# Feed-forward part and output projection of a hybrid layer by 2 x 2 blocks in seven half-size products, with weight sums made by DMAs

## The chip, the cores and the metric

One Trainium2 chip, one core of it. The metric is the device time of one execution in microseconds, the median of several runs. A core has a matrix engine (TensorE, PE in the profile; the loading of its stationary operand is listed apart as PEld), VectorE (DVE), ScalarE (ACT), GpSimd (POOL) and SyncE (SP). Each takes its instructions in order and waits on semaphores for the others. DMAs are issued from the stream of an engine, here nearly all from SP (kind "hardware_dynamic" in the list of queues) and some from POOL ("software_dynamic").

## The reference

One layer, depth 1, in fp32, on 2048 prompt tokens and 8 x 4 decode tokens, width 1024, feed-forward width 3072:

```
xn   = rms_norm(x, g_mix_norm);  proj = xn @ w_in
mix  = concat(pooling mixer, RG-LRU recurrence, cross-attention into 256 memory tokens), each rms-normalised
x    = x + (mix * g_mix_out) @ w_out                       # 1024 x 1024
xn   = rms_norm(x, g_ffn_norm)
gate = xn @ w_ff_gate;  up = xn @ w_ff_up                  # 1024 x 3072 each
gate = gelu(causal depthwise conv of width 3 over gate)
x    = x + (gate * up) @ w_ff_down                         # 3072 x 1024
y    = rms_norm(x, g_final)
```

The states of the pooling, the convolutions and the recurrence are outputs too. The three products of the feed-forward part hold most of the arithmetic.

## The kernel before

**Arithmetic.** Activations lie with the channel on the 128 partitions and the token on the free axis. An fp32 product is made of three: both operands are split into a high part that the matrix engine's fast fp32 form takes whole and a low rest (`split`, L123 on ACT for the high part, L124 on VectorE or GpSimd for the rest), and `acc3` (L219 to L223) adds hi*hi, hi*lo and lo*hi into one PSUM tile.

**Tiling.** The 2080 columns are 6 pieces of 344, 344 and four times 348, taken in 3 blocks b of two pieces. A matmul has a 128 x 128 piece of a weight as its stationary operand and one piece of columns as the moving one.

**Stages.** First the recurrent group (input projection, convolution, gates, recurrence) of all 6 pieces, to some 290 us; then pooling and cross-attention, to some 530 us; the results lie in DRAM as mix. The output projection of block 0 covers the end of these groups (478 to 558 us). Then for each block: the output projection (blocks 1 and 2), the residual, the norm, and a loop over 24 chunks f of 128 feed-forward channels. A chunk loads 512 KB each of `w_gate`, `w_up`, `w_down` on SP and splits them 1024 wide, makes 48 matmuls for the gate and 48 for the up product, the conv on VectorE (L1042, L1047, L1054), the gelu on ACT, and the product of both (`hp`). The norm factor is multiplied in after the products, so these start without it. The 8 steps of the down product of a chunk (6 matmuls each) are kept in a list and popped between the matmuls of the next chunk; each adds its PSUM tile into `y` on VectorE (L893).

**The end.** The last chunk goes by halves of the columns (`last_down`), so that the norm and the stores of the first half run under the second.

**What sets the order.** Matmuls and SP's loads run in the written order; in the first two groups a weaver places background steps by a table of times `W`, which the change does not touch. The order on VectorE, ACT and POOL is chosen by the framework's scheduler from its own estimates, and a DMA issued from POOL is an instruction in POOL's order: if it has to wait for an earlier DMA, what stands behind it on POOL waits too.

## Time and profile before

| | |
|---|---|
| median of 3 runs | 2374.73 us (2374.39 to 2375.63) |
| span of the profiled execution | 2372.1 us |
| PE busy | 2298.0 us, 97%, 14370 matmuls |
| VectorE busy | 1640.9 us, 69% |
| ScalarE busy | 724.8 us, 31% |
| GpSimd busy | 484.5 us, 20% |
| moved by DMA | 195.88 MB, 83 GB/s over the span |
| granted clock of PE, mean | 0.986 |

The time of the profiled execution itself is not listed apart from its span; the median of the runs is 2.6 us above the span, which I take as what lies around it. In the rows below, a group of instructions shows `out<-in`, the count, the busy time and the mean of one in ns, then the idle time of that engine just before them and what ended it. A row of windows gives for a stretch of the span the busy time and the number of instructions of each engine, then the granted clock (1.00 is full), the share of time that the 16 DMA engines were busy, and GB/s.

### The profile page before, as it was taken

How to read it: one execution, taken by the hardware profiler on the slowest of the kernel's cores; microseconds unless marked ns; L12 is line 12 of the kernel's file. 1: busy time of each engine (PE TensorE's matmuls, PEld its weight loads, DVE VectorE, ACT ScalarE, POOL GpSimd, SP SyncE). 2: the span in 40 equal slices, each digit the busy share in tenths (PEclk: the TensorE clock that was granted, in tenths of full speed). 3: DMA queues.
4: the chain of work that ended last, by engine and by line, in shares of the span. 5: the costliest groups of instructions: out<-in, count | busy, mean ns of one | idle time of the engine just before them, and what ended most of it. 6: DMA issues, size and time to landing. Idle time of an engine off the chain costs nothing.

```text
span 2372.1 us, 34512 instructions
## 1 busy us (share of the span) xinstructions
PE 2298.0 (97%) x14370; PEld 2242.8 (95%) x14370; DVE 1640.9 (69%) x2404; ACT 724.8 (31%) x1016; POOL 484.5 (20%) x438
## 2 busy tenths in 40 slices
PE   8899889999999999999999999999999999999997
PEld 7888788889999999999999999999999999999996
DVE  8897886766666666666676666666658666666666
ACT  6646554644212212123421221212143121221212
POOL 3332343322111111101411011111132111111112
PEclk9899999999999999999999999999999999999998
DMA  4012332144222222224332222222163222222201
GB/s 157 26 49 81 117 148 82 61 146 128 70 72 72 63 79 65 71 63 150 103 109 69 72 63 75 68 72 72 35 195 111 72 72 63 72 64 79 71 20 49
DMA packets 60124, 195.88 MB, mean 83 GB/s; under 512 B 6832, under 2 KB 15776, under 8 KB 59968
## 3 DMA queue, kind: packets, MB, share of 16 engines
q1 hardware_dynamic: 55488, 177.96, 23.9%
q0 software_dynamic: 4336, 15.64, 1.7%
q8 instruction: 112, 1.84, 0.3%
q14 instruction: 44, 0.36, 0.1%
q10 hardware_dynamic: 144, 0.09, 0.0%
HBM read 175.17 MB, written 18.49 MB: 82 GB/s over the span
## 4 chain that ended last, share of the span: by engine, by line
PE 78%; DVE 14%; issue 3%; ACT 2%; POOL 2%; DMA 1%; DVEq 0%; SPq 0%; ACTq 0%; POOLq 0%
PE pu L223 22%; PE pd L223 22%; PE pg L223 22%; PE po L223 5%; PE pq L223 2%; DVE xc L511 2%; DVE alr L129 1%; PE pg L437 1%; DVE xc L508 1%; DVE xc L538 1%; DVE e L614 1%; DVE qu L801 1%; PE pf L223 1%; DVE y L907 1%; DVE m L606 1%
## 5 line engine op out<-in xcount | busy, mean ns | idle before, releaser
L893 DVE TENSOR_TENSOR y<-pd,y 128x696 f32<-128x696 f32 (+1 forms) x568 | 497.4, 876 | 422.5 <-PE pd L223 422.0
L223 PE MATMUL pd<-hh,h_wd 128*128 128x348 f32 (+1 forms) x1152 | 279.8, 323 | 2.8 <-DVE y L893 1.2
L223 PE MATMUL pg<-aha,l_wg 128*128 128x348 f32 (+1 forms) x1152 | 278.8, 322 | 0.0
L223 PE MATMUL pg<-aha,h_wg 128*128 128x348 f32 (+1 forms) x1152 | 278.7, 322 | 0.0
L223 PE MATMUL pu<-aha,h_wu 128*128 128x348 f32 (+1 forms) x1152 | 278.6, 322 | 0.0
L223 PE MATMUL pd<-hh,l_wd 128*128 128x348 f32 (+1 forms) x1152 | 278.6, 322 | 0.0
L223 PE MATMUL pg<-ala,h_wg 128*128 128x348 f32 (+1 forms) x1152 | 278.2, 321 | 0.0
L223 PE MATMUL pd<-hl,h_wd 128*128 128x348 f32 (+1 forms) x1152 | 277.4, 321 | 0.7 <-DVE hl L124 0.6
L223 PE MATMUL pu<-aha,l_wu 128*128 128x348 f32 (+1 forms) x1152 | 277.6, 321 | 0.0
L223 PE MATMUL pu<-ala,h_wu 128*128 128x348 f32 (+1 forms) x1152 | 277.0, 320 | 0.0
L1041 POOL COPY halo<-gt 128x2 f32<-128x2 f32 x72 | 67.2, 934 | 1002.1 <-DVE gt L1039 991.6
L123 ACT ACTIVATE h_wu<-st_wu 128x1024 fp32r<-128x1024 f32 x72 | 76.4, 1061 | 484.4 <-PE pg L223 483.6
L223 PEld LDWEIGHTS pd<-hh,h_wd 128*128 128x128 f32 x1152 | 200.2, 188 | 4.9 <-DVE y L893 1.8
L223 PEld LDWEIGHTS pd<-hl,h_wd 128*128 128x128 f32 x1152 | 199.9, 188 | 1.5 <-DVE hl L124 1.5
L223 PEld LDWEIGHTS pg<-ala,h_wg 128*128 128x128 f32 x1152 | 200.9, 189 | 0.0
L223 PEld LDWEIGHTS pu<-ala,h_wu 128*128 128x128 f32 x1152 | 200.6, 189 | 0.0
L223 PEld LDWEIGHTS pd<-hh,l_wd 128*128 128x128 f32 x1152 | 200.4, 188 | 0.0
L223 PEld LDWEIGHTS pu<-aha,h_wu 128*128 128x128 f32 x1152 | 200.1, 188 | 0.0
L223 PEld LDWEIGHTS pg<-aha,l_wg 128*128 128x128 f32 x1152 | 200.0, 189 | 0.0
L223 PEld LDWEIGHTS pg<-aha,h_wg 128*128 128x128 f32 x1152 | 199.7, 188 | 0.0
L223 PEld LDWEIGHTS pu<-aha,l_wu 128*128 128x128 f32 x1152 | 199.1, 188 | 0.0
L1056 ACT ACTIVATE cv<-cv,pv 128x696 f32<-128x696 f32 (+2 forms) x73 | 63.4, 868 | 431.8 <-DVE cv L1047 304.3
(337 smaller groups left out, 4049.4 us busy)
## 6 DMA issues: line engine op xcount, KB each, us to landing
st_wg<-in_w_gate_dram SPq DMA_DIRECT2D x72, 512.0 KB, 3.6
st_wu<-in_w_up_dram SPq DMA_DIRECT2D x72, 512.0 KB, 3.6
st_wd<-in_w_down_dram SPq DMA_DIRECT2D x72, 512.0 KB, 3.6
st_wo<-in_w_out_dram SPq DMA_DIRECT2D x24, 512.0 KB, 5.4
xr<-in_x_dram SPq DMA_DIRECT2D x8, 696.0 KB, 4.7
xp<-in_x_dram SPq DMA_DIRECT2D x8, 696.0 KB, 5.6
y<-in_x_dram SPq DMA_DIRECT2D x16, 348.0 KB, 5.5
st_wr<-in_w_in_dram SPq DMA_DIRECT2D x7, 512.0 KB, 4.6
```

What stands on the lines that cost most here:

```text
L123: S.activation(out=hi, in_=src, func=AF.Copy)
L129: V.scalar_tensor_tensor(out=lo, in0=src, scalar=g, in1=hi.bitcast(F32), op0=ALU.mult, op1=ALU.subtract)
L223: T.matmul(o, w_[:, ks], z, start=(k == 0 and i == 0), stop=(k == nk - 1 and i == 2))
L437: T.matmul(pg[:, 0:n], bdg[:, 4 * d + c, :], xc[:, c, :], start=True, stop=True)
L508: V.tensor_scalar(out=xc[:, c, p0:n], in0=xr[:, j, 3:3 + npr], scalar1=pcol("rcw", 4 * c + 3), scalar2=pcol("rcb", c), op0=ALU.mult, op1=A ...
L511: V.scalar_tensor_tensor(out=xc[:, c, p0:n], in0=xr[:, j, i:i + npr], scalar=pcol("rcw", 4 * c + i), in1=xc[:, c, p0:n], op0=ALU.mult, op1 ...
L538: V.tensor_tensor_scan(out=xc[:, c, p0:n], data0=a[:, c, p0:n], data1=ii[:, c, p0:n], initial=h_prev[:, c:c + 1], op0=ALU.mult, op1=ALU.add)
L606: V.tensor_reduce(out=m4[:w, i:i + v.shape[1]], in_=v, op=ALU.max, axis=AX.X)
L614: V.tensor_scalar(out=e[:w, h, :], in0=e[:w, h, :], scalar1=m4[:w, 8 + h:9 + h], scalar2=None, op0=ALU.mult)
L893: V.tensor_tensor(out=y[d], in0=pt[:, :, 0:n], in1=y[d], op=ALU.add)
L1041: G.tensor_copy(halo[:, f, :], gt[:, nn:nn + 2])
L1056: S.activation(out=cv[:, c0:c1], in_=cv[:, c0:c1], func=AF.Gelu_apprx_tanh, bias=pcol("fcb", f))
```

## The change

**Blocks.** The three feed-forward products of all blocks and the output projection of blocks 1 and 2 are no longer made tile by tile. A step takes a 2 x 2 block form: the weight's 1024 x 256 piece as 4 blocks (2 halves of the inner dimension, 2 output chunks), the activations as 4 blocks (2 halves of the inner dimension, 2 pieces of columns), and makes Strassen's seven products in Winograd's form. A product is 4 inner chunks times 3 split terms, 12 matmuls; a step is 84 matmuls for what took 96. The output projection of block 0 stays.

**Sums of weights.** Four of the seven products need a sum of weight blocks (`s1` to `s4`). For gate and up a sum is 3.15 MB, for the output projection a third of that, for down 3.15 MB. They are built in DRAM by POOL's queue: per weight four copies from DRAM to DRAM and four DMAs that add onto their destination, in six steps (`sums`) of which the later ones need the earlier ones' results. The steps for gate, up and out are written into the loops over the pieces of the first two groups, those for down into steps 5 to 15 of the first block's gate and up stage. `w_down` is first laid out anew in DRAM by `relay`: three times 16 DMAs on SP of 256 KB in runs of 512 bytes.

**Loads.** A product's weight is a 256 KB piece, loaded on SP and split 512 wide, six products ahead. `h` (gate times up) goes to DRAM and comes back as blocks for the down stages, as does the output projection's result `ys`. A stage loads its block of activations (2.85 MB) in the last steps of the stage before.

**Activations.** The seven forms of the activations (`early`, `prep`) are made and split once per stage, in the last steps of the stage before. The norm is now applied to the block before the products (`normalise`, 8 instructions), the sums of squares are added from whole quads (`add_squares`), and their column sums (`stat`) and the spreading of the factor are popped one and four products behind the last product that feeds them.

**PSUM and the end.** A step has four banks of its eight; results are combined by `post`. The last block's end no longer goes by halves of the columns.

**Order of stages:** ffn 0 (gate and up), down 0 of block 0, output projection 1, down 1 and 2 of block 0, ffn 1, and so on.

The diff, cut to its core (the old feed-forward loop, its chunk-wise down steps and the split end are removed):

```diff
+    def pair_blocks(w):
+        v = w.rearrange("(q i) p (j k) -> i j p q k", i=2, j=2)
+        return {(i + 1, j + 1): v[i, j] for i in range(2) for j in range(2)}
+    WB, WS = {}, {}
+    for nm, wn in (("gate", "w_gate"), ("up", "w_up"), ("out", "w_out")):
+        WB[nm] = pair_blocks(I[wn])
+    WB["down"] = {(i, j): dr.tile([P, 12, 512], F32, name=f"wd{i}{j}") for i in (1, 2) for j in (1, 2)}
+    for nm in WB:
+        q = 4 if nm == "out" else 12
+        WS[nm] = [dr.tile([P, q, 512], F32, name=f"ws_{nm}{i}") for i in range(4)]
+    def sums(nm, step):
+        a, (s1, s2, s3, s4) = WB[nm], WS[nm]
+        todo = (((s1, a[2, 1], 0), (s3, a[1, 1], 0)), ((s1, a[2, 2], 1), (s3, a[2, 1], 1)), ((s2, s1, 0),),
+                ((s2, a[1, 1], 1),), ((s4, s2, 0),), ((s4, a[1, 2], 1),))[step]
+        for d, z, add in todo:
+            if add:
+                G.dma_start(out=d[:, :, :], in_=z[:, :, :], accum_op=ALU.add, max_dma_last_dim=8192)
+            else:
+                G.dma_start(out=d[:, :, :], in_=z[:, :, :])
+    def relay(g):
+        v = I["w_down"].rearrange("(g x k) p (j i m) -> g x i j p k m", g=3, x=2, k=4, j=4, i=2)
+        for x in range(2):
+            for i in range(2):
+                for j in range(4):
+                    nc.sync.dma_start(out=WB["down"][i + 1, x + 1][:, 4 * g + j, :].rearrange("p (k m) -> p k m", k=4),
+                                      in_=v[g, x, i, j])
...
+        for nm, t in (("gate", s - 1), ("up", s - 2)):
+            if 0 <= t < 6:
+                sums(nm, t)
...
+        for nm, t in (("gate", s + 5), ("up", s + 4), ("out", s)):
+            if 0 <= t < 6:
+                sums(nm, t)
...
+        NWT, AHEAD = 8, 6
...
-            def step(d):
-                pt = psB(f"pd{b}_{f}_{d}")
-                acc3(halves(pt, n), w, ks_(d), [[z[:, h, :] for h in range(2)] for z in hp], 0, 1)
-                V.tensor_tensor(out=y[d], in0=pt[:, :, 0:n], in1=y[d], op=ALU.add)
...
+        def quad(name, w=0):
+            return fp.tile([P, 2, 2 + 2 * WMAX], F32, tag="c", bufs=3, name=name)
...
+            def early(self):
+                q = self.q
+                self.X = fp.tile([P, 4, self.n], F32, tag="x", bufs=1, name="x" + self.name)
+                V.tensor_tensor(out=q[1, 2], in0=q[1, 2], in1=q[1, 1], op=ALU.subtract)
+                V.tensor_tensor(out=self.X, in0=q[1, 2], in1=q[2, 2], op=ALU.subtract)
+            def prep(self, i):
+                q, X = self.q, self.X
+                src, sign = ((X, 1), (q[1, 1], 1), (q[1, 2], -1), (q[1, 1], -1), (X, 1), (q[2, 1], 1), (q[2, 2], 1))[i]
+                self.s[i] = [fp.tile([P, 4, self.n], F32R, tag=f"{z}{i}", bufs=1, name=f"{z}{i}{self.name}") for z in "hl"]
+                split_s(self.s[i][0], self.s[i][1], src, sign)
+                if i == 1:
+                    V.tensor_tensor(out=q[1, 1], in0=q[1, 1], in1=X, op=ALU.add)
+                    V.tensor_tensor(out=X, in0=X, in1=q[2, 1], op=ALU.add)
...
+        def forms(nm, q):
+            a, s = WB[nm], WS[nm]
+            return [z[:, q, :] for z in (s[1], a[1, 1], s[0], s[2], a[2, 2], a[1, 2], s[3])]
...
+            def product(self, i, blk, wt):
+                n = blk.n
+                if i == 0:
+                    self.b = [bank(f"{z}{self.name}") for z in "bacd"]
+                pb, pa_, pc, pdd = self.b
+                pt = (pb, pa_, pc, pb, pdd, pa_, pc)[i]
+                hi, lo = blk.s[i]
+                for k in range(4):
+                    for z, (w_, a_) in enumerate(((0, hi), (0, lo), (1, hi))):
+                        T.matmul(pt[:, 0:n], wt[:, w_, ks_(k)], a_[:, k, :], start=(i in (0, 1, 2, 4) and k == z == 0),
+                                 stop=(k == 3 and z == 2), skip_group_check=True)
+            def post(self, i, n):
+                pb, pa_, pc, pdd = (z[:, 0:n] for z in self.b)
+                o = self.out
+                if i == 0:
+                    self.t6 = short("t6" + self.name, n)
+                    S.activation(out=self.t6, in_=pb, func=AF.Copy)
+                elif i == 1:
+                    self.t1 = short("t1" + self.name, n)
+                    S.activation(out=self.t1, in_=pa_, func=AF.Copy, scale=-1.0)
+                    V.tensor_tensor(out=self.t6, in0=pa_, in1=self.t6, op=ALU.add)
+                elif i == 3:
+                    V.tensor_tensor(out=self.t1, in0=self.t1, in1=pb, op=ALU.subtract)
+                    V.tensor_tensor(out=o(2, 2), in0=self.t1, in1=pc, op=ALU.subtract)
+                elif i == 4:
+                    V.tensor_tensor(out=o(2, 1), in0=pdd, in1=self.t1, op=ALU.add)
+                elif i == 5:
+                    S.activation(out=o(1, 1), in_=pa_, func=AF.Copy)
+                elif i == 6:
+                    V.tensor_tensor(out=o(1, 2), in0=pc, in1=self.t6, op=ALU.add)
+                    if self.done:
+                        self.done()
...
+            return [stat] + [lambda: None] * 2 + [bcast]
...
+                def done_up(j=j, k=k):
+                    u = qv(k["u"], n)
+                    G.tensor_tensor(out=u, in0=u, in1=qv(k["cv"], n), op=ALU.mult)
+                    G.dma_start(out=hs[b][j // 4][:, 2 * (j % 4):2 * (j % 4) + 2].rearrange("p f h t -> p f (h t)"), in_=u)
...
+        def load_wt(x):
+            si, ti, i = prods[x]
+            src = stages[si][2][ti].w[i]
+            raw = fp.tile([P, 512], F32, tag="wr", bufs=5, name=f"wr{x}")
+            nc.sync.dma_start(out=raw, in_=src)
+            w = fp.tile([P, 2, 512], F32R, tag="wt", bufs=NWT, name=f"wt{x}")
+            split(w[:, 0], w[:, 1], raw)
+            wts[x] = w
...
+        normalise(blk, RBN[0][0])
+        blk.early()
+        for x in range(AHEAD):
+            load_wt(x)
+        for i in range(7):
+            blk.prep(i)
+        nxt = None
+        for x, (si, ti, i) in enumerate(prods):
+            kind, b, steps, _ = stages[si]
+            if x + AHEAD < len(prods):
+                load_wt(x + AHEAD)
+            st = steps[ti]
+            if i == 0 and st.begin:
+                st.begin()
+            st.product(i, blk, wts.pop(x))
+            st.post(i, blk.n)
+            pop()
+            if si + 1 < len(stages):
+                at = len(steps) - 3 if kind != "ffn" else 11
+                if ti == at and i == 3:
+                    nxt = stages[si + 1][3]()
+                    nkind, nb = stages[si + 1][:2]
+                if ti == len(steps) - 2 and i == 3:
+                    if nkind == "ffn":
+                        normalise(nxt, RBN[nb][0])
+                    nxt.early()
+                if ti == len(steps) - 1:
+                    nxt.prep(i)
+                    if i == 6:
+                        blk = nxt
...
+                if b == 0 and i == 0:
+                    if ti in (1, 2, 3):
+                        relay(ti - 1)
+                    elif ti in (5, 7, 9, 11, 13, 15):
+                        sums("down", (ti - 5) // 2)
...```

**The order of the instructions, first place:** POOL in the recurrent group, from the gates of the third piece of columns on. `i_` is a gate's product, `sqr` the squares for a norm, `xc` the convolved input, `mixr<-g` the store of a piece's result; `ws_gate`, `ws_up` are the sums of weights. Before:

```order
L440 TENSOR_TENSOR i_613<-i_613,xc_611 128x344 x4
L334 TENSOR_TENSOR sqr_973<-sqr_973 128x1392
L336 TENSOR_TENSOR sqr_973<-sqr_973 128x696
L312 TENSOR_TENSOR xc_611<-xc_611 128x688
L336 TENSOR_TENSOR sqr_973<-sqr_973 128x348
L312 TENSOR_TENSOR xc_611<-xc_611 128x344
L321 DMA mixr_78<-g_403 512x1x344
```

And now:

```order
L480 TENSOR_TENSOR i_635<-i_635,xc_633 128x344 x3
L217 DMA ws_gate_86<-ws_gate_85 48x16384
L480 TENSOR_TENSOR i_635<-i_635,xc_633 128x344
L215 DMA ws_up_89<-in_w_up_dram 1536x1x512
L215 DMA ws_up_91<-in_w_up_dram 1536x1x512
L374 TENSOR_TENSOR sqr_999<-sqr_999 128x1392
L215 DMA ws_gate_86<-in_w_gate_dram 1536x1x512
L376 TENSOR_TENSOR sqr_999<-sqr_999 128x696
L361 DMA mixr_75<-g_423 512x1x344
L376 TENSOR_TENSOR sqr_999<-sqr_999 128x348
```

L217 is the plain copy, L215 the adding one. The scheduler has set them between the gates and the norms of the recurrent group: the first copy, `ws_gate_85<-in_w_gate_dram`, stands right behind the start of POOL's stream, and all of them for gate, up and the output projection stand ahead of the split of the memory weights, `l_wkv`.

**Second place:** SP early in the first block's gate and up stage. `st_` are the old whole weight loads, `wr` the new half-size ones, `wd` the new layout of `w_down`. Before:

```order
L136 DMA st_wg_1_5509<-in_w_gate_dram 128x1024
L136 DMA st_wu_1_5515<-in_w_up_dram 128x1024
L136 DMA st_wd_1_5521<-in_w_down_dram 128x1024
L136 DMA st_wg_2_5706<-in_w_gate_dram 128x1024
L136 DMA st_wu_2_5712<-in_w_up_dram 128x1024
```

And now:

```order
L1217 DMA wr_5669<-ws_up_92 128x512
L225 DMA wd_81<-in_w_down_dram 128x4x128 x4
L225 DMA wd_83<-in_w_down_dram 128x4x128 x4
L225 DMA wd_82<-in_w_down_dram 128x4x128 x4
L225 DMA wd_84<-in_w_down_dram 128x4x128 x4
L1217 DMA wr_5709<-ws_gate_86 128x512
L1217 DMA wr_5729<-in_w_gate_dram 128x512
```

The 16 DMAs of one `relay` stand between two weight loads, three times.

**Third place:** POOL in the first block's gate and up stage. `halo` and `dctx` keep the conv's context, `cv` and `u` are the gelu's and the up product's tiles, `hs` is h in DRAM. Before:

```order
L1041 COPY halo<-gt_1_5527 128x2
L1051 COPY dctx<-gt_1_5527 128x8x4
L1057 TENSOR_TENSOR cv_1_5528<-cv_1_5528,rbfa_5401 128x688
L1041 COPY halo<-gt_2_5724 128x2
L1051 COPY dctx<-gt_2_5724 128x8x4
L1057 TENSOR_TENSOR cv_2_5725<-cv_2_5725,rbfa_5401 128x688
```

And now:

```order
L1096 COPY halo<-gt_1_5826 128x4
L217 DMA ws_down_99<-wd_81 48x16384
L1122 TENSOR_TENSOR u_1_5992<-u_1_5992,cv_1_5971 128x2x688
L217 DMA ws_down_97<-wd_83 48x16384
L1123 DMA hs_5335<-u_1_5992 128x2x688
L1109 COPY dctx<-gt_2_6144 128x8x4
L215 DMA ws_down_97<-wd_84 384x2048
L1096 COPY halo<-gt_2_6144 128x4
L1109 COPY dctx<-gt_2_6144 128x8x4
L215 DMA ws_down_99<-wd_83 384x2048
L1122 TENSOR_TENSOR u_2_6294<-u_2_6294,cv_2_6273 128x2x688
L217 DMA ws_down_98<-ws_down_97 48x16384
```

The sums for down stand between the products that finish `u` and the copies of the gate's last columns; all eight stand ahead of the first such product behind `halo<-gt_4`, some six steps on from `halo<-gt_1`.

More of the change, by code (lines that the diff above doesn't have):

```diff
@@ new lines, in blk_ffn, with blk_out, blk_down @@
+        def blk_ffn(b):
+            return load_block(f"a{b}", NCOL[2 * b], [ys[b]])
+        def blk_out(b):
+            return load_block(f"o{b}", NCOL[2 * b], [mix_p[b][:, 0:2], mix_r[b], mix_p[b][:, 2:4]])
+        def blk_down(b, g):
+            return load_block(f"d{b}{g}", NCOL[2 * b], [hs[b][g]])
+        stages = []
+        for b in range(NBLK):
+            stages.append(("ffn", b, ffn_stage(b), lambda b=b: blk_ffn(b)))
+            for g in range(3):
+                stages.append(("down", b, down_stage(b, g), lambda b=b, g=g: blk_down(b, g)))
+                if g == 0 and b + 1 < NBLK:
+                    stages.append(("out", b + 1, out_stage(b + 1), lambda b=b: blk_out(b + 1)))
@@ new lines, in hybrid_kernel @@
+        prods = [(si, ti, i) for si, st in enumerate(stages) for ti in range(len(st[2])) for i in range(7)]
+        wts = {}
+        def load_wt(x):
[6 more added lines that the diff above has]
+            wts[x] = w
+        n = NCOL[0]
```

399 lines of the change are left out of this document (194 added, 205 removed).

## The prediction

> **What bounds the kernel now.** I read the page first, then the chain of waits, then windows by stage.
>
> ```profile
> span 2372.1 us, 34512 instructions
> PE 2298.0 (97%) x14370; PEld 2242.8 (95%) x14370; DVE 1640.9 (69%) x2404; ACT 724.8 (31%) x1016; POOL 484.5 (20%) x438
> PE 78%; DVE 14%; issue 3%; ACT 2%; POOL 2%; DMA 1%; DVEq 0%; SPq 0%; ACTq 0%; POOLq 0%
> ```
>
> PE is busy for 97% of the span and holds 78% of the chain; VectorE holds the 14% that are left over in the early groups.
>
> ```profile
> core 0: us, PE busy (x) PEld busy (x) DVE busy (x) ACT busy (x) POOL busy (x), PEclk, DMA share, GB/s
> 0.00:239.00 239.00, 210.69 (x1183) 193.39 (x1184) 203.78 (x404) 141.64 (x177) 82.61 (x58) 0.94 0.22 78
> 540.00:1100.00 560.00, 557.54 (x3537) 556.95 (x3536) 371.07 (x471) 123.69 (x136) 78.63 (x79) 1.00 0.23 70
> 1100.00:1700.00 600.00, 598.65 (x3767) 598.03 (x3767) 394.75 (x457) 142.71 (x158) 97.74 (x91) 1.00 0.27 84
> 1700.00:2300.00 600.00, 598.53 (x3770) 597.90 (x3769) 395.52 (x457) 143.21 (x159) 98.33 (x91) 1.00 0.27 82
> ```
>
> From 540 us on PE is never idle, at the full granted clock, and the other engines have a third of their time free. A matmul costs 560/3537 = 0.158 us there, 600/3767 = 0.159 in the later two. So a matmul saved in this stretch is 0.159 us saved, if the others keep up. The first 239 us are another matter: PE is idle for 28 us, VectorE is at 85%, and all three helpers wait for one another; a delay of POOL there has little to hide behind.
>
> **The change, part by part.** All terms are against the profiled span of 2372.1 us; the median of the runs, 2374.7, is 2.6 more.
>
> *A, fewer matmuls.* Before, gate, up and down have 1152 matmuls per split term:
>
> ```profile
> L223 PE MATMUL pg<-aha,l_wg 128*128 128x348 f32 (+1 forms) x1152 | 278.8, 322 | 0.0
> L893 DVE TENSOR_TENSOR y<-pd,y 128x696 f32<-128x696 f32 (+1 forms) x568 | 497.4, 876 | 422.5 <-PE pd L223 422.0
> ```
>
> That is 9 x 1152 = 10368; at 84 for 96 it becomes 9072, 1296 fewer. The output projection of two blocks has 768, 96 fewer. 1392 x 0.159 = **-221 us**.
>
> *B, the start of the feed-forward part.* The products can no longer start ahead of the norm. The rows:
>
> ```profile
> L333 ACT ACTIVATE sqr<-xr 128x1392 f32<-128x1392 f32 x8 | 10.4, 1351 | 0.0
> 566.59 1.39 PE L161 MATMUL sfa<-ones,ss 128*86 128x1 f32 x16 [2.22 <-POOL ss L873]
> 568.01 0.16 DVE L165 TENSOR_SCALAR vvfa<-sfa 86x8 f32<-86x8 f32 x1 [0.74 <-PE sfa L161]
> 569.99 0.16 DVE L152 SCALAR_TENSOR_TENSOR rsfa<-thfa,rsfa 86x8 f32<-86x8 f32 x1
> L1047 DVE SCALAR_TENSOR_TENSOR cv<-gt,pv,cv 128x696 f32<-128x696 f32 x94 | 87.8, 934 | 0.1
> L124 DVE TENSOR_TENSOR l_wu<-st_wu,h_wu 128x1024 fp32r<-128x1024 f32 x72 | 94.8, 1317 | 1.5 <-ACT h_wu L123 1.4
> L933 DVE TENSOR_TENSOR y<-pd,y 128x348 f32<-128x348 f32 x16 | 8.1, 517 | 5.2 <-PE pd L223 5.2
> ```
>
> In a row: the last residual 0.9, its squares 1.35, column sums by 64 matmuls 4 x 1.39 = 5.6, the root 570.15 - 568.01 = 2.1, spreading it 1.5 (estimate: as long as the sums of one tile), eight normalising instructions 8 x 0.93 = 7.5, two differences of 1376 columns at about 1.6 each (1317 ns for 1024, scaled between that and 0.93 for 696), the first form's split 1.35 + 1.6: 25. The other six splits, 9.7, and two sums, 3.2, fall into the first step beside 7 x 0.66 of weight splits and 5 x 0.52 of results: 20 us on VectorE where PE needs 84 x 0.159 = 13.4. **+32** together; below that no less than 25.
>
> *C, norms between stages.* The column sums are queued one product (12 x 0.159 = 1.9 us) behind the last result, but need VectorE 0.5, POOL's addition, ACT's squares 1.35, and POOL's two additions:
>
> ```profile
> L334 POOL TENSOR_TENSOR sqr<-sqr 128x1392 f32<-128x1392 f32 x4 | 16.1, 4027 | 58.2 <-ACT sqr L333 29.2 <-DVE xc L538 14.7 <-DVE hcar L543 14.3
> L873 POOL TENSOR_TENSOR ss<-ss,sqfa 128x696 f32<-128x696 f32 x14 | 31.7, 2265 | 4.6 <-ACT sqfa L872 4.5
> ```
>
> 0.5 + 4.0 + 1.35 + 2 x 2.3 = 10.4, so PE stands for 8 us, at four places (two blocks' output projection, two blocks' final norm): **+32**. The products behind them stand in PE's order and cannot pass.
>
> *D, turns to the next block.* From the middle of the last step but one to the end of the next stage's first, 33.5 us of PE, VectorE has: normalising 7.5, two differences 3.2, seven splits 11.6, two sums 3.2, 17 weight splits 11.2, 12 results 6.2, some of the final factor 2.8: 46. Half of the excess is covered by weights split six products ahead: 6 at two turns, **+12**. At turns to a down or projection stage the first and last drop out, 35.4 against 33.5, and I take nothing. In steady work the conv is to be added:
>
> ```profile
> L1042 DVE TENSOR_SCALAR cv<-gt,pv 128x688 f32<-128x688 f32 x24 | 13.7, 570 | 0.0
> L1054 DVE SCALAR_TENSOR_TENSOR cv<-dctx,pv,cv 128x32 f32<-128x32 f32 x48 | 11.8, 245 | 0.0
> ```
>
> A gate step of block 0 has 4.6 + 2.6 + 2 x (0.57 + 2 x 0.93) + 4 x 0.25 = 13.0 of 13.4, an up step 7.2: hidden, with little over.
>
> *E, the end.*
>
> ```profile
> L223 PE MATMUL pd<-hh,l_wd x1152: 315/322/331, 584.4 to 2352.6; 128*128 128x348 f32 x128, 128*128 128x344 f32 x64
> out_y_dram<-y POOLq DMA_DIRECT2D x8, 348.0 KB, 3.5
> ```
>
> Before, 19.2 us follow the last matmul (2372.1 - 2352.9). After, C's chain 10.4, sums and root 3.5, spreading 1, eight factors 7.5, the last store 3.5: 26. **+6**.
>
> *F, the sums of gate, up and projection.* No copy from DRAM to DRAM and no adding DMA is in the trace. The nearest rows:
>
> ```profile
> DMA packets 2062, 6.48 MB, mean 381 GB/s; under 512 B 388, under 2 KB 644, under 8 KB 2060
> st_wg<-in_w_gate_dram SPq DMA_DIRECT2D x72, 512.0 KB, 3.6
> 238.63 2.46 POOL L124 TENSOR_TENSOR l_wkv<-st_wkv,h_wkv 128x1024 fp32r<-128x1024 f32 x1 [14.29 <-ACT h_wkv L123]
> ```
>
> With all DMA engines loaded (295 to 312 us) they moved 381 GB/s. A sum of 3.15 MB at that rate is 8.3 us. A copy is between that (as a load) and twice it, 16.6 (read, then write); an adding DMA between 8.3 and three times it, 24.9 (two reads, one write). Nothing tells which, so I take the middles: copy 12.4, adding 20.7. Four of each for gate and up and a third for the projection are 9.33 x 33.1 = 309 us of DMA, all ahead of `l_wkv` in POOL's order, which ran at 238.6. The last adding one, 6.9, need not be waited for; the loads of the window, 0.22 x 239 = 53, share the engines; the idle time of POOL there, 14.3, gives some 8 back. 309 - 6.9 + 53 - 238.6 - 8 = **+109**. From bounds: 0 (155 + 53 is less than 238.6) to 185.
>
> *G, the new layout of w_down.* 512-byte runs; the nearest row is a queue of 625-byte packets at the start:
>
> ```profile
> q10 hardware_dynamic: 144, 0.09, 0.6%
> ```
>
> 0.6% of 16 engines x 60 us over 144 packets is 40 ns each. 16 DMAs of 512 runs are 8192 x 40 ns / 16 = 20.5 us. Weight loads stand behind them on SP; four products ready, 8 us, cover some: 12.5 x 3 = **+37**. From 3 each (4.19 MB at 381 GB/s, 11, less 8), 9, to 33 each (every run handled twice), 99.
>
> *H, the sums of down* stand in six steps of POOL's order, 80 us of PE. Four copies and three adding ones, 4 x 12.4 + 3 x 20.7 = 112, and 42 weight loads of 0.69, 29, less 80 and 9 that `u` may be late: **+52**; from 0 to 81.
>
> *I, the clock.*
>
> ```profile
> 298.29 0.43 PE L223 MATMUL pf<-alp,h_wq 128*128 128x344 f32 x1 [3.09 <-DVE alp L129]
> 301.81 0.49 PE L223 MATMUL pf<-ahp,h_wq 128*128 128x344 f32 x1
> 300.00:305.00 5.00, 3.93 (x14) 3.94 (x15) 5.00 (x6) 3.12 (x5) 3.46 (x3) 0.50 1.03 404
> ```
>
> After gaps of 3 and 2 us PE ran five at half clock, a loss of 2 to 2.5. Some 12 such gaps in B to H: **+24**; 10 to 30.
>
> Sum: -221 + 32 + 32 + 12 + 6 + 109 + 37 + 52 + 24 = +83. 2372.1 + 83 + 2.6 = **2458 us**, slower.
>
> The two prices of F and H carry this. The Trainium skill, "Collectives: The Full Stack", section "The bandwidth ceiling: the fold count and why AG ≠ RS ≠ AR", says that a reducing transfer goes at half a copy's speed, since both its reads go through one ring; with the copy at 12.4 that would be 24.8 and 2507 us in all. "DMA: Bandwidth & Descriptors", section "Latency and other measured facts", has 207 to 214 GB/s for copies between HBM tensors; a copy would be about 15 us, and with the adding price kept, some 2495. No run here shows either.
>
> **The rivals.** *R1: the sums hide.* The DMA engines work at 0.22 to 0.27 and have room; if a copy and an adding DMA cost what a load costs, F and H are nothing: -221 + 82 + 9 (G) + 10 = -120, 2255 us. For it: the low share of DMA. Against: each handles its bytes at least twice.
>
> *R0: two reads count, the write is free* (8.3 and 16.6). F: 9.33 x 24.9 - 5.5 + 53 - 246.6 = 33; H: 33 + 50 + 29 - 89 = 23; G 37, clock 20: -221 + 82 + 33 + 23 + 37 + 20 = -26, 2349 us, faster.
>
> *R2: each pass over memory follows the other* (16.6 and 24.9): F 185, H 81, G 99, clock 30: +256, 2631 us. The stores between memories would have to show no overlap, as to which the trace is silent.
>
> It decides at a copy plus an adding DMA of 26 us: above it the waits of POOL in F and H eat the 221, below it the change is faster.
>
> **How the numbers follow.** The forecast, 2385 to 2540 with its own prices, 0.37; R2 0.21; R0 0.19; R1 0.19; near the balance 0.04. Faster is R0 and R1, 0.38; slower the forecast and R2, 0.58; no change, within 0.2% (about what a measurement of this kernel tells from nothing), 0.04. The range 2250 to 2640 takes in the four results and leaves out what lies beyond the bounds, like doubled F with G.
>
> **What would show it.** A: from the first block's down stage on, 0.159 us for each of fewer matmuls, PE at 97% or more, granted clock 1.00. B: some 25 us with PE idle before the first gate product. C: four gaps of 8 us with the column sums released by POOL's `ss`. F: POOL's adding DMAs waiting for earlier DMAs, `i`, `sqr` and `xc` behind them late, and `l_wkv` near 350 us instead of 238.6. G: weight splits released by `wr` loads after each of three groups of SP DMAs. H: `u` released late on POOL in steps 3 to 9 of the first gate and up stage. E: 26 us behind the last matmul. Wrong it would be if the l_wkv split kept its time, if a copy and an adding DMA together took under 26 us, or if PE between 700 and 2200 us were held by VectorE, which I have at 13.0 of 13.4 in the fullest step.

## The result and the profile after

The changed kernel takes 2526.5 us (median of 4 runs, 2523.1 to 2528.6) where the kernel before takes 2374.6: a ratio of 1.064, 95% interval 1.062 to 1.066, so 152 us slower. The forecast was 83 us slower. The page of the changed kernel begins with its span and the busy times of the engines:

```profile
span 2526.5 us, 35620 instructions
PE 2169.7 (86%) x13048; PEld 2101.0 (83%) x13048; DVE 1847.8 (73%) x2865; ACT 1135.5 (45%) x1895; POOL 642.0 (25%) x456
```

PE has 1322 instructions fewer by its count (13048 for 14370) and is busy for 128 us less, but its share falls from 97% to 86%. Windows by stage show where the rest went (stretch; length; busy time of PE, PEld, VectorE, ScalarE, GpSimd; granted clock; DMA share; GB/s):

```profile
0.00:298.00 298.00, 223.38 (x1214) 204.56 (x1215) 203.66 (x403) 141.30 (x175) 104.43 (x81) 0.88 0.98 256
617.00:653.00 36.00, 19.55 (x136) 19.15 (x136) 14.76 (x26) 12.10 (x14) 0.00 (x0) 0.54 0.24 84
640.00:1082.00 442.00, 343.32 (x2019) 337.82 (x2018) 283.90 (x441) 169.88 (x287) 62.25 (x67) 0.88 0.72 220
1082.00:1360.00 278.00, 232.47 (x1367) 228.62 (x1366) 212.56 (x256) 129.34 (x198) 87.78 (x34) 0.91 0.50 170
1360.00:1700.00 340.00, 325.54 (x2034) 324.95 (x2034) 273.72 (x389) 159.84 (x274) 62.34 (x56) 0.98 0.55 178
```

The first row holds the early groups with the sums under way, and 0.98 is the share of the DMA engines. The second is the uncovered start of the feed-forward part. The third and the last are the same work, the gate and up stage of blocks 0 and 1: 442 us, with 13 of waiting at its start, and 340. The fourth is the three down stages and the projection between them. What PE waited for, summed by line:

```profile
PE cd L1012 <- DVE cd L1027: 54.2, 15, 7.8
PE str L160 <- POOL sqr L376: 35.9, 4, 15.1
PE bg L1012 <- ACT wt L122: 31.5, 2, 28.1
PE sfn L160 <- POOL sn L1048: 29.3, 3, 10.9
PE bg L1012 <- ACT t6g L1020: 22.2, 3, 13.4
PE sfa L160 <- POOL sa L1048: 22.2, 2, 11.1
PE co L1012 <- DVE co L1027: 18.4, 4, 7.8
PE cu L1012 <- DVE u L1027: 14.3, 4, 4.4
PE bg L1012 <- ACT h0a L122: 13.1, 1, 13.1
```

The columns are the total in us, the times, and the longest. `cd`, `co` and `cu` waiting for VectorE (54.2 + 18.4 + 14.3 = 87 us) are the turns between stages; `sfn` and `sfa` the column sums (51.5, of which 8.3 at the very end); `bg` for `wt` and `t6g` the first gate and up stage; `h0a` its start. `str` are the column sums of the recurrent group's norm, which wait for POOL's squares: 35.9 us here, all within the first 298 us, and 2.6 in the kernel before.

The split of the memory weights on POOL, which the prediction had put near 350 us, ran at 298.2; before it ran at 238.6:

```profile
298.23 2.46 POOL L123 TENSOR_TENSOR l_wkv<-st_wkv,h_wkv 128x1024 fp32r<-128x1024 f32 x1 [0.73 <-PE pr L263]
```

### The profile page after: what moved, and what is told of

Same layout as the page of the kernel before. It is cut to its first block, busy times and chain, and to the rows that moved or that the text cites. A ratio compares the mean times of both kernels' runs of the same rounds, so it can differ in the third digit from the quotient of the medians.

```text
span 2526.5 us, 35620 instructions
## 1 busy us (share of the span) xinstructions
PE 2169.7 (86%) x13048; PEld 2101.0 (83%) x13048; DVE 1847.8 (73%) x2865; ACT 1135.5 (45%) x1895; POOL 642.0 (25%) x456
## 3 DMA queue, kind: packets, MB, share of 16 engines
q0 software_dynamic: 31696, 133.64, 19.2%
## 5 line engine op out<-in xcount | busy, mean ns | idle before, releaser
L123 DVE TENSOR_TENSOR wt<-wr,wt 128x512 fp32r<-128x512 f32 x812 | 697.8, 871 | 272.3 <-ACT wt L122 268.8
L122 ACT ACTIVATE wt<-wr 128x512 fp32r<-128x512 f32 x812 | 503.4, 627 | 518.9 <-DMA wr<-ws_gate 56.1
L1142 POOL TENSOR_TENSOR Y<-Y,cd 128x1392 f32<-128x1392 f32 (+1 forms) x36 | 132.3, 3676 | 400.4 <-ACT wt L122 243.0
L1122 POOL TENSOR_TENSOR u<-u,cv 128x1392 f32<-128x1392 f32 (+1 forms) x36 | 123.4, 3428 | 402.3 <-DVE u L1033 201.1
L1012 PE MATMUL cd<-h6d,wt 128*128 128x348 f32 (+1 forms) x288 | 89.4, 377 | 54.2 <-DVE cd L1027 54.2
L1105 DVE SCALAR_TENSOR_TENSOR cv<-gt,pv,cv 128x696 f32<-128x696 f32 (+2 forms) x144 | 132.8, 923 | 1.1
L1012 PE MATMUL bg<-h0a,wt 128*128 128x348 f32 (+1 forms) x288 | 79.2, 339 | 44.6 <-ACT wt L122 31.5
L1012 PEld LDWEIGHTS cd<-h6d,wt 128*128 128x128 f32 x288 | 62.1, 228 | 58.4 <-DVE cd L1027 58.4
L1012 PE MATMUL bg<-h3a,wt 128*128 128x348 f32 (+1 forms) x288 | 78.8, 337 | 22.7 <-ACT t6g L1020 22.2
L1012 PEld LDWEIGHTS bg<-h0a,wt 128*128 128x128 f32 x288 | 54.3, 201 | 45.9 <-ACT wt L122 32.1
L1012 PE MATMUL cu<-h6a,wt 128*128 128x348 f32 (+1 forms) x288 | 78.4, 336 | 14.3 <-DVE u L1027 14.3
L263 PE MATMUL pr<-ahr,h_wr 128*128 128x348 f32 (+1 forms) x192 | 65.5, 341 | 19.2 <-ACT ahr L127 9.4
L1012 PE MATMUL bu<-h0a,wt 128*128 128x348 f32 (+1 forms) x288 | 75.7, 326 | 7.1 <-ACT wt L122 7.1
L1012 PE MATMUL bu<-h3a,wt 128*128 128x348 f32 (+1 forms) x288 | 76.3, 328 | 6.1 <-ACT t6u L1020 6.1
L1012 PE MATMUL ag<-h5a,wt 128*128 128x348 f32 (+1 forms) x288 | 75.5, 325 | 6.7 <-DVE t6g L1024 6.7
L1012 PE MATMUL ag<-h1a,wt 128*128 128x348 f32 (+1 forms) x288 | 79.1, 338 | 0.0
L1115 ACT ACTIVATE cv<-cv,pv 128x696 f32<-128x696 f32 (+1 forms) x72 | 62.6, 872 | 36.6 <-DVE cv L1105 20.7
L1012 PE MATMUL bd<-h0d,wt 128*128 128x348 f32 (+1 forms) x288 | 78.8, 338 | 0.0
L1012 PE MATMUL cg<-h6a,wt 128*128 128x348 f32 (+1 forms) x288 | 75.6, 325 | 3.4 <-DVE gt L1027 3.4
L1012 PE MATMUL ad<-h1d,wt 128*128 128x348 f32 (+1 forms) x288 | 77.3, 331 | 0.0
L1012 PE MATMUL ad<-h5d,wt 128*128 128x348 f32 (+1 forms) x288 | 74.5, 322 | 2.5 <-DVE t6d L1024 2.5
L1012 PE MATMUL cd<-h2d,wt 128*128 128x348 f32 (+1 forms) x288 | 75.2, 324 | 0.0
```

The costliest lines, as they stand in the source:

```text
L122: S.activation(out=hi, in_=src, func=AF.Copy)
L123: (eng or V).tensor_tensor(out=lo, in0=src, in1=hi.bitcast(F32), op=ALU.subtract)
L263: T.matmul(o, w_[:, ks], z, start=(k == 0 and i == 0), stop=(k == nk - 1 and i == 2))
L1012: T.matmul(pt[:, 0:n], wt[:, w_, ks_(k)], a_[:, k, :], start=(i in (0, 1, 2, 4) and k == z == 0), stop=(k == 3 and z == 2), skip_group_che ...
L1105: V.scalar_tensor_tensor(out=cv[:, z0:nn], in0=gt[:, z0 + t:nn + t], scalar=pcol("fcw", 3 * f + t), in1=cv[:, z0:nn], op0=ALU.mult, op1=AL ...
L1115: S.activation(out=cv, in_=cv, func=AF.Gelu_apprx_tanh, bias=pcol("fcb", f))
```

## The experiments

Each starts from the changed kernel unless another is named. One profiled run each, beside the kernel before on the same chip, save the last kernel, which was timed in three rounds.

### The price of a sum's DMA, alone and side by side

The kernel before, with this behind its last store (`copy` and `acc` as in `sums`, each tied to the one before it by a small DMA or by its operand):

```diff
+ copy(s1, vw[1, 0]); acc(s1, vw[1, 1]); copy(s2, s1); acc(s2, vw[0, 0])
+ copy(s3, vw[0, 0]); copy(s4, vw[1, 0])      # side by side
+ 8 x nc.sync.dma_start(...)                  # of the 48 of relay
```

> The kernel before, with DMAs added behind its last store, one waiting for the other: a copy of 3.15 MB from DRAM to DRAM out of the weight's blocks, an adding DMA of the same, a copy from one sum to the next, an adding DMA, then two copies side by side, then eight of the 48 DMAs that lay w_down anew. In the changed kernel the POOL queue's packets take 19.2% of 16 engines' span, 485 us; less the stores in it, some 420 us for 26.7 sums' DMAs, 15.8 us each. Theory 1, a copy's and an adding DMA's prices differ as in the prediction's middles: copy 12.4 us, adding 20.7. Rival, bytes alone count: 15.8 both. Rival, an adding DMA is twice a copy: 10.5 and 21. Two copies side by side take twice one if the engines are the limit, and as long as one if latency is. The eight DMAs of the new layout: 10 us by the prediction's 40 ns a run, 5.5 us by their bytes.

The DMAs on POOL, with their start, and in brackets how long POOL waited for the one before:

```profile
2371.16 1.00 POOL L1085 DMA_DIRECT2D xs<-in_w_gate_dram  x1 [2.13 <-DMA xs<-y]
2384.48 1.75 POOL L1088 DMA_DIRECT2D xs<-in_w_gate_dram  x1 [12.31 <-DMA xs<-in_w_gate_dram]
2404.78 0.53 POOL L1085 DMA_DIRECT2D xs<-xs  x1 [18.56 <-DMA xs<-in_w_gate_dram]
2417.61 1.71 POOL L1088 DMA_DIRECT2D xs<-in_w_gate_dram  x1 [12.30 <-issue]
2437.95 1.09 POOL L1094 DMA_DIRECT2D xs<-xs  x2 [18.63 <-DMA xs<-in_w_gate_dram]
2440.73 2.00 POOL L1085 DMA_DIRECT2D xs<-in_w_gate_dram  x2 [1.69 <-DMA xs<-xs]
2463.51 1.21 SPq L1098 DMA_DIRECT2D xs<-xs  x2
```

From start to start a copy takes 13.3 and 12.8 us, an adding DMA 20.3 and 20.3. The prediction's middles were 12.4 and 20.7, and its other price for a copy, some 15, is too high. The rivals in which bytes alone count, and in which a copy takes 10.5, fall. Two copies side by side are done after 22.8 us (SP's small DMA at 2463.5 waits for the second), nearer to two alone, 26.1, than to one. The eight DMAs of the new layout, on SP's queue, took 7.0 us to issue, and the span ended 11.8 us after the first, near the 10 of the prediction's price:

```profile
2465.63 7.01 SPq L1102 DMA_DIRECT2D xs<-in_w_down_dram  x8
```

The Trainium skill, "Collectives: The Full Stack", section "The bandwidth ceiling: the fold count and why AG ≠ RS ≠ AR", has a reducing transfer at half a copy's speed, measured there for collectives between cores; here the ratio is 20.3/13.0 = 1.56, so the measurement decides against the full factor of two in this kernel.

A second such kernel has pairs side by side, and weight loads beside a copy and an adding DMA:

```diff
+ copy(s3, vw[0, 0]); copy(s4, vw[1, 0]); acc(s3, vw[1, 1]); acc(s4, vw[1, 1])
+ copy(d1, vw[0, 0]); acc(d1, s4)             # with 30 loads of 256 KB on SP beside them
```

> The kernel before with DMAs behind its last store: a copy of 3.15 MB, a copy from sum to sum, two copies side by side, two adding DMAs side by side, then one copy and one adding DMA with 30 weight loads of 256 KB beside them. Alone, a copy took 13 us and an adding DMA 20. Theory, the early groups had room for 9.33 pairs in 300 us because adding DMAs side by side share the time that one leaves unused: two take 28 to 32 us instead of 40, and two copies 23. Rival, the engines are full with one: two take 40. Weight loads beside them: landing 12 to 20 us instead of 3 if they stand behind the sums' packets, 3 to 5 if the queues share.

```profile
2398.61 2.01 POOL L1085 DMA_DIRECT2D xs<-in_w_gate_dram  x2 [1.50 <-DMA xs<-xs]
2413.82 1.76 POOL L1088 DMA_DIRECT2D xs<-in_w_gate_dram  x1 [13.19 <-issue]
2422.30 1.70 POOL L1088 DMA_DIRECT2D xs<-in_w_gate_dram  x1 [6.72 <-DMA xs<-in_w_gate_dram]
2454.86 1.02 POOL L1085 DMA_DIRECT2D xs<-in_w_gate_dram  x1 [30.86 <-DMA xs<-xs]
```

Two copies end after 23.7 us (2398.6 to 2422.3), where one after the other would take 26. The first adding DMA starts at 2413.8, behind the first copy and beside the second. SP's next DMA, which waits for both adding ones, is issued at 2452.6. So two copies and two adding DMAs took 54.0 us together, where the prices alone give 2 x 13.0 + 2 x 20.3 = 66.6: 27 us a pair instead of 33, as the theory had it. The weight loads, while the last copy ran (2454 to 2472 us), while the last adding DMA ran (2472 to 2495), and after both (2495 to 2512), with the median time to landing:

```profile
stx<-in_w_gate_dram SPq DMA_DIRECT2D x10, 256.0 KB, 5.4
stx<-in_w_gate_dram SPq DMA_DIRECT2D x7, 256.0 KB, 11.2
stx<-in_w_gate_dram SPq DMA_DIRECT2D x14, 256.0 KB, 3.2
```

So one large DMA is enough to make small loads late: 5.4 us beside a copy and 11.2 beside an adding DMA, for 3.2 after both. Of the seven beside the adding DMA the slowest took 19.7 us; the 12 to 20 expected are reached by some of them.

### Without the sums for gate, up and output projection

```diff
-            if 0 <= t < 6:
-                sums(nm, t)
+            if nm != "down":  s = (a[2, 1], a[2, 2], a[1, 1], a[1, 2])   # in forms()
```

> The changed kernel without the sums for gate, up and output projection; the products that need a sum read a block of the weight instead, at the same size. This leaves out part of the computation. Theory, the sums cost the early groups what the trace shows (the last residual of block 0's projection ends at 617 us instead of 558): 2526 - 59 = 2467 us, l_wkv's split back near 239 us. Rival, the prediction's term F of 109: 2417. Rival, the time is lost at the weight loads that the sums crowd, and comes back only in part: over 2490.

2466 us: 60 come back, all of what the trace showed. The first product of the feed-forward part starts at 593.9 us for 653.4, and `l_wkv` is back at its old place:

```profile
237.41 2.45 POOL L123 TENSOR_TENSOR l_wkv<-st_wkv,h_wkv 128x1024 fp32r<-128x1024 f32 x1 [14.30 <-ACT h_wkv L122]
```

The term F of the prediction, 109, is refuted in size.

### POOL in the written order

```diff
-    ctx.enter_context(tc.manual_schedule(engines={mybir.EngineType.SP}))
+    ctx.enter_context(tc.manual_schedule(engines={mybir.EngineType.SP, mybir.EngineType.Pool}))
```

> The changed kernel with POOL's instructions in the written order, in which the sums' DMAs stand some 40 us apart, down to the last piece of the cross-attention, instead of all ahead of l_wkv. The same bytes move. Theory, the 59 us of the early groups come from POOL waiting for DMAs in its order: 40 of them go, 2486 us. Rival, they come from loads that are late while the DMA engines are full: spreading the sums gives as much. Against both, if the sums only move the wait into the cross-attention: 2526. The two theories are told apart by what the early waits name as their releaser, and by the idle time of POOL ahead of its DMAs.

2512 us: 14 come back, so none of the three numbers held. Of these, the early groups give only 4 (the first product of the feed-forward part starts at 649.7 us for 653.4) and the first gate and up stage 9 (419.6 us from its first product on, for 428.8). In the changed kernel POOL waited for sums at eight places by more than 4 us each, from 160 us on, 76 us in sum, such as

```profile
171.77 0.56 POOL L217 DMA_DIRECT2D ws_gate<-ws_gate  x1 [11.11 <-DMA ws_gate<-in_w_gate_dram]
183.83 1.76 POOL L215 DMA_DIRECT2D ws_up<-in_w_up_dram  x1 [9.64 <-DMA ws_up<-ws_up]
192.68 1.69 POOL L215 DMA_DIRECT2D ws_gate<-in_w_gate_dram  x1 [7.09 <-DMA ws_gate<-ws_gate]
193.60 7.26 POOL L374 TENSOR_TENSOR sqr<-sqr 128x1392 f32<-128x1392 f32 x1
```

The last line is the first part of the squares for a norm, which stood behind these waits; PE waited 10.6 us for the last part, until 205.9. Of the 35.9 us that PE waited for such squares, 14 come behind POOL's waits for sums (at 205.9 and 248.4), and 22 before the first of them (at 92.9 and 147.3). Those 22 fit loads and stores that are late while the DMA engines are full. In the changed kernel's first 298 us:

```profile
q0 software_dynamic: 18656, 59.93, 82.8%
q1 hardware_dynamic: 4464, 15.99, 14.5%
xr<-in_x_dram SPq DMA_DIRECT2D x8, 696.0 KB, 7.8
st_wkv<-in_wkv_dram SPq DMA_DIRECT2D x3, 512.0 KB, 15.4
```

The same loads of 696 KB took 4.7 us to land before, the weights of the memory 8.2. But this run changes the whole order of POOL, so it doesn't separate the two causes cleanly; the last two runs below add to it.

### Without the new layout and the sums for down, and without the layout alone

```diff
-                    if ti in (1, 2, 3):
-                        relay(ti - 1)
-                    elif ti in (5, 7, 9, 11, 13, 15):
-                        sums("down", (ti - 5) // 2)
+            if nm == "down":  a = WB["gate"]; s = (a[2, 1], a[2, 2], a[1, 1], a[1, 2])   # in forms()
```

> The changed kernel without the new layout of w_down and without the sums for down; the down products read blocks of the gate's weight instead, at the same size. This leaves out part of the computation. Theory, these two cost what the first gate and up stage is longer than the second: 441.9 - 13.1 (its start) - 342.2 = 87 us, so 2526 - 87 = 2439 us, and the stage takes about 355 us with its start. By the prediction's terms G and H, 89, and the clock's share behind their gaps, about 8: 2429. Rival, the stage is long because block 0's conv brings VectorE to its limit: under 20 us are gained.

2436 us, 91 less, half clock behind the gaps included: G and H together had been put at 89, and 97 with the clock's share. The rival, that block 0's conv brings VectorE to its limit, falls. For the second kernel `w_down` is handed in as blocks, so that `relay` goes and the scheduler sets the sums for down under the cross-attention:

```diff
-    WB["down"] = {(i, j): dr.tile([P, 12, 512], F32, name=f"wd{i}{j}") for i in (1, 2) for j in (1, 2)}
+    WB["down"] = {(i, j): I["w_down"][i - 1, j - 1] for i in (1, 2) for j in (1, 2)}
```

> The changed kernel with w_down handed in as blocks, so that no new layout is made on the chip; the scheduler then sets the sums for down into POOL's order ahead of and under the cross-attention. Theory, the gaps at 690 to 760 us (3.4 + 7.1 + 28.1 = 39) are the new layout's and go; those from 800 us on (13.4 + 5.7 + 2.9 + 4.7 + 6.1 + 4.1 = 37) are those of the sums and move into the early groups, where half is hidden: 2526 - 39 - 37 / 2 - 10 of clock = 2459 us. Rival, the prediction's G alone: 37, 2489. Rival, all of the sums' time comes back in the early groups, as the DMA engines are full there: 2526 - 39 - 5 = 2482, with the first product of the feed-forward part some 37 us later than 653.

2463 us, where 2459 was expected. The first gate and up stage falls from 441.9 to 345.4 us, and starts at 673.6 instead of 640.4: the stage has lost all of its extra time, and the early groups have gained 33 us, nearly the 37 of gaps that were put down to the sums. So hardly any of it is hidden there, and that 2463 is near the 2459 expected is luck in part: half of the sums' time was to be hidden, and the half clock that went with the gaps is 17 us instead of 10.

How the two hold up the stage is in the changed kernel's trace. SP's own queue, with the time that the issuing takes, and the product that waited:

```profile
671.50 13.29 SPq L225 DMA_DIRECT2D wd<-in_w_down_dram  x16
694.09 15.28 SPq L225 DMA_DIRECT2D wd<-in_w_down_dram  x16
717.30 35.20 SPq L225 DMA_DIRECT2D wd<-in_w_down_dram  x16
758.62 0.65 PE L1012 MATMUL bg<-h0a,wt 128*128 128x344 f32 x1 [28.12 <-ACT wt L122]
```

Sixteen DMAs of 512 runs keep SP busy issuing for 13 and 15 us, and for 35 the third time, while two copies for the sums, issued at 725.1 and 734.2 us, are under way; the weight loads behind them are not even issued. PE waited 3.4, 7.1 and 28.1 us behind the three. For the sums, the loads issued between 780 and 808 us, beside two adding DMAs, with the median time to landing:

```profile
wr<-ws_up SPq DMA_DIRECT2D x3, 256.0 KB, 27.1
wr<-in_w_up_dram SPq DMA_DIRECT2D x3, 256.0 KB, 22.1
```

They land after 16 to 35 us, where 3 is the median of the whole run, longer than the six products (11 us) that are loaded ahead. And a late load also stops what it is not for. ScalarE, which splits the weights, takes its instructions in order, and `t6g`, the copy that frees the bank which the fourth product of the step writes, stood behind the split of a weight for the following step:

```profile
805.52 0.63 ACT L122 ACTIVATE wt<-wr 128x512 fp32r<-128x512 f32 x1 [5.61 <-DMA wr<-ws_up]
806.05 0.44 ACT L1020 ACTIVATE t6g<-bg 128x344 f32<-128x344 f32 x1
806.54 0.66 PE L1012 MATMUL bg<-h3a,wt 128*128 128x344 f32 x1 [13.42 <-ACT t6g L1020]
```

### Late column sums

```diff
-            bg.extend([lambda: None] + norm_steps(...))
+            bg.extend([lambda: None] * 7 + norm_steps(...))
```

> The changed kernel with the column sums between stages popped seven products behind the last result instead of one. Theory, PE stands at four places for POOL's additions, 11.1 + 10.2 + 11.1 + 10.9 = 43 us, plus some 2 us of half clock behind each: 2526 - 50 = 2476 us. Rival, the products in between wait for POOL or VectorE too, so that the gap only moves: within 10 us of 2526. At the end of the kernel nothing changes, as nothing stands between.

2499 us, 28 less, not 50. The four waits of 11.1, 10.2, 11.1 and 10.9 us are gone, but the stages behind them get only 3 to 10 us shorter each (145.4 to 137.1, 342.2 to 338.9, 146.8 to 136.5, 343.4 to 336.6). Part of the time is lost elsewhere again: PE's waits for `cd` rise from 54 to 59 us, and 530 matmuls instead of 478 take over 0.2 us from start to start, where 0.159 is the full pace. That the waits had let the other engines catch up fits this, but no run shows it.

### No new forms at 9 of 11 turns

```diff
+                    if nxt.n != blk.n:
                         nxt.early()
...
+                    if nxt.n != blk.n:
                         nxt.prep(i)
+                    else:
+                        nxt.s[i] = blk.s[i]
```

> The changed kernel in which 9 of the 11 turns between stages make no new forms of the activations but use the old ones (wherever the width is the same); loads and norms stay. This leaves out part of the computation. Theory, VectorE's work on the forms holds up PE in the last step of each stage (PE waits 54 + 18 + 14 + 3 us for results of VectorE at product 6) and each wait is followed by some us of half clock: 9/11 of 90 + 25, so 2526 - 94 = 2432 us. Rival, the prediction's term D: 12 us, 2514. Rival, the loads of the blocks (2.85 MB) hold up the turn: no change, 2526.

2430 us, 96 less, where 94 was expected and 12 by the prediction's term D. The run takes away ScalarE's part of the forms too; that VectorE's part is what counts is read from the releasers of PE's waits. In the last step of a stage in the changed kernel, once the first form is being split (at 1343.3 us here), VectorE is not idle any more, and the results that PE waits for stand between the splits of the next forms:

```profile
1353.31 0.50 DVE L1026 TENSOR_TENSOR t1d<-t1d,bd 128x344 f32<-128x344 f32 x1
1353.73 1.59 DVE L950 SCALAR_TENSOR_TENSOR l3a<-R0a,h3a 128x1392 fp32r<-128x1392 f32 x1
1355.25 0.50 DVE L1027 TENSOR_TENSOR cd<-t1d,cd 128x344 f32<-128x344 f32 x1
```

Product 6 writes the bank that `cd` at 1355.25 still has to read; PE stood for 7.8 us until then.

### Three edits together

```diff
+ w_down as blocks, column sums seven products late, POOL in the written order
```

> Three edits together: w_down handed in as blocks, the column sums seven products late, POOL in the written order. If they add up: 2526 - 28 (measured for the column sums) - 87 - 40 = 2371 us, level with the kernel before. If the sums for down, which now stand in the first gate and up stage without the new layout ahead of them, still hold POOL there: 2400.

2456 us, 85 above the sum of the parts. With POOL in the written order the sums for down stand in the first gate and up stage again; it takes 406.5 us, 71.8 of it idle, though POOL waits for none of them there. The weight loads beside the sums are late here too, such as these between 725 and 760 us:

```profile
wr<-ws_up SPq DMA_DIRECT2D x4, 256.0 KB, 17.6
```

So in this stage it is loads late beside the sums, and not POOL waiting in its order.

### Seven products for gate and up alone

By the run without new forms a turn costs 96 / 9 = 10.7 us; a stage of four steps saves 48 matmuls, 7.6 us. This kernel undoes half of the change: down and output projection by plain blocks, with no sums, no layout and four forms instead of seven, whose buffers come free half a step earlier.

```diff
-                steps.append(Step(f"d{b}{g}{j}", "down", ...))
+                steps.append(PlainStep(f"d{b}{g}{j}", "down", ...))     # w11, w21, w12, w22; 24 matmuls each
-                sums("down", (ti - 5) // 2)
+        sums(("gate", "up")[s % 2], s // 2)                             # one step to each piece of columns
```

> Half of the change undone: seven products for gate and up alone, down and output projection by plain 2 x 2 blocks (four weights, 96 matmuls a step, no sums, no new layout, four forms instead of seven), POOL in the written order with the sums' twelve steps spread one to each piece of columns, column sums four or seven products late. From the changed kernel: 44 steps with 12 matmuls more, 44 x 1.9 = +84; no sums for down and no new layout, -87; the column sums -28; the turns to plain stages as without new forms, -85; the early groups -30 to -45 of 59. 2526 - 146 to 161, so 2365 to 2380: level with the kernel before, 2374. If plain turns stall as the old ones: 2450. If the spread sums cost nothing any more: 2355.

2338 us, a ratio of 0.984 to the kernel before (0.982 to 0.986): 1.6% faster than that kernel, and faster than any of the numbers expected. The page, and the down stages of block 0 with the projection between them:

```profile
span 2334.7 us, 35594 instructions
PE 2192.6 (94%) x13576; PEld 2135.6 (91%) x13576; DVE 1658.2 (71%) x2524; ACT 1002.9 (43%) x1686; POOL 604.5 (26%) x440
963.00:1208.00 245.00, 245.00 (x1559) 244.98 (x1558) 141.69 (x135) 80.09 (x120) 74.46 (x34) 1.00 0.45 146
```

The same work took 278 us in the changed kernel with 192 matmuls fewer (267 with the column sums late, by its four stages). In this stretch PE is now busy throughout at the full clock. From the first product of the feed-forward part on it waits 33 us in all, for 224 in the changed kernel, and 64 matmuls instead of 478 take over 0.2 us. Several edits act together here, so what each is worth is not shown apart.

Two runs ask what the early groups still lose. First with POOL's order left to the scheduler again, then without sums:

```diff
-    ... engines={mybir.EngineType.SP, mybir.EngineType.Pool}
+    ... engines={mybir.EngineType.SP}
```

> The mixed kernel (seven products for gate and up alone, 2338 us) with POOL's order left to the scheduler again, which sets all sixteen sums' DMAs ahead of l_wkv. The first product of the feed-forward part starts at 634.6 us in the mixed kernel. Theory, packing the same DMAs into the first 250 us costs the early groups what spreading saved: 14 us as measured in the changed kernel, 2352. Rival, spread or packed is the same, as the bytes are: 2338. Rival, the written order itself costs POOL something, so that the scheduler's is better: under 2338.

2340 us: no difference that one run can tell, though the sixteen DMAs are packed into the early part; the first product starts at 641.0 us for 634.6. In the total the rival holds. What is behind it shows in the next run.

```diff
-        sums(("gate", "up")[s % 2], s // 2)
```

> The mixed kernel without any sums; the products that need one read a block of the weight at the same size. This leaves out part of the computation. Before the change the last residual ahead of the feed-forward part was done at about 558 us, in the mixed kernel at about 598. Theory, the spread sums cost these 40 us still: 2298, first product at 595. Rival, a good part of the 40 is POOL's written order, not the sums: 2320.

2309 us: the sums of gate and up cost 29 us, and the first product still starts at 605.6 us. It started at 593.9 with no sums and the scheduler's order, so the written order costs some 12 by itself, as the rival said. With the scheduler's order the packed sums of gate and up cost 641.0 - 593.9 = 47 us, with the written order the spread ones 634.6 - 605.6 = 29. So spreading saves some 18, and the order takes 12 of them: that is why it looked useless. These are single runs. In the mixed kernel POOL waits for none of the sums' DMAs in the early groups, and still they cost 29, so not all of their price is POOL waiting in its order.

## Why the prediction was right, and where it was wrong

The direction, the range and the likeliest case's own range held, but in good part by luck. The sum of 83 was short of the 154 between the spans: F was 50 and G with H 13 too large, while D was some 80, I some 36, B and C together 24 and E 3 too small. The prediction let the price of a pair of DMAs decide, with the balance at 26 us. With the 27 that a pair took together, its own sum gives F 52 and H 31, and with 82 for B to E, 37 for G and some 21 for the clock -221 + 82 + 52 + 31 + 37 + 21 = +2: no change. That the kernel became slower all the same came most of all from D and I, which the sum had at 36. One of the prediction's signs of being wrong was seen, too: between 700 and 2200 us VectorE held PE for some 73 us, at the turns and not in the gate step that it had looked at; and in the first down stages (1082 to 1360 us) PE was at 84% instead of 97, with the clock at 0.91.

- **A, -221: held.** Where nothing is late, in the window of the mixed kernel above, 1559 instructions took 245.0 us, 0.157 each. The profile has 1322 fewer instead of 1392: B's column sums add 112, and the other small steps of the norms are 42 fewer.
- **B, +32: 45.** From the last residual (617.0) to the first product (653.4) 36 us, and 8 more in the first step, of which some 4 are half clock that stands in I as well. The step that failed is the column sums. I read the row of 16 as 16 of the written matmuls; it was 8, as each shows twice. So the 64 show as 128, and on top they ran while the granted clock was 0.54:

```profile
619.63 17.10 PE L160 MATMUL sfa<-ones,sq 128*86 128x1 f32 x116 [0.57 <-ACT sq L1230]
653.42 0.65 PE L1012 MATMUL bg<-h0a,wt 128*128 128x344 f32 x1 [13.06 <-ACT h0a L122]
```

- **C, +32: 43 of waiting,** with POOL's additions (`sa` and `sn`) as the releaser, as said; taken away it was worth 28.
- **D, +12: about 90 of waiting, 96 with 9 of 11 turns removed.** This is the largest miss. The step was "at turns to a down or projection stage ... I take nothing": it weighed VectorE's work over 2.5 steps and let the surplus average out. The forms' buffers come free one product at a time in the last step, so the work is packed there: 7 splits and 2 sums of 1.6 us, 7 weight splits of 0.68 and 5 results of 0.5, 21.7 us against 13.4, and the results stand behind the splits.
- **E, +6: 9.** 28.3 us behind the last product (2498.2 to 2526.5), 19.2 before.
- **F, +109: 59.** The middles for a copy and an adding DMA were right (13.0 and 20.3 for 12.4 and 20.7). The mis-sized step is the multiplication of their sum by 9.33 as if each ran alone. Together a pair takes 27: in the changed kernel the POOL queue took 0.828 x 298 = 247 us for the 9.33 pairs less the last adding DMA (9.33 x 27 - 6 = 246), where the sum had 302. That takes 55 off; the loads took 0.145 x 298 = 43 for 53. With both the sum gives 44; what the other 15 are is not shown. As for the mechanism, POOL did wait in its order as said, and PE behind it for 14 us, but the loads were late too, which the prediction had as a load on the engines alone. How the 59 divide between these two is open, since no run held POOL's order fixed while it moved the DMAs.
- **G and H, +89: 76 of waiting,** 39 behind the new layout and 37 beside the sums; 91 with the half clock, which the sum had in I. In H the mechanism was wrong. I had `u` late on POOL, and no wait of PE names POOL's `u`; it was weight loads late beside the sums, and results behind their splits on ScalarE. In G the loads stood behind SP's issuing, 13, 15 and 35 us for 16 DMAs, where I had priced transfers.
- **I, +24: some 60.** From 617 us on, 478 matmuls took over 0.2 us from start to start where 0.159 is the full pace, 65 us more than that; before, 44 from 558 us on, 5 us. There were 43 gaps of over 1 us from 617 us on where I had counted 12, many of them D's.

The measured parts, -221 + 45 + 43 + 90 + 9 + 59 + 76 + 60, give 161 for the 154 between the spans, 4 of which are counted twice. R1 falls on the price of a pair, 16.6 for 27, and R2 with 41.5. R0's 24.9 was nearer to 27 than my own 33.1. What kept the kernel from R0's 2349 is first D and I, 118 more than the 32 that R0 has for them; F and H with G came to 42 more.

## What to carry to other kernels

Seven products for eight save a fixed share of a step and pay once per stage, so count the steps: a stage of four saves 48 matmuls, 7.6 us, and its turn cost more than that here, while one of 24 saves 46 us for one turn, so the same change gains in one stage and loses in the other. When buffers come free one by one, weigh the helper's work over the stretch in which it may be done, not over a stage. A large background DMA also costs through the small loads that land late beside it, here 11 us and more; ask whether the loads are issued further ahead than that, and whether results wait on the same engine behind the split of a weight that has not landed. No run here tried to load further ahead or to move these splits.
